# Seven block products in place of eight in part of a down projection (float32 trunk kernel, one Trainium2 core)

## The chip, the core and the metric

One NeuronCore of a Trainium2 chip runs the whole program. The metric is the device time of one execution in microseconds (us); for the kernel before it is the median of three timed executions. Beside these stands one profiled execution, with a trace of every engine.

## The reference

Two residual layers over a sequence of 256 tokens of width 2048, all in float32. Each layer has three kinds of attention heads and then a gated MLP with a causal convolution. The change lies in the MLP's last product:

```python
def _conv_gated_mlp(h, w_up, conv_w, conv_b, w_down):
    u = jnp.einsum('bsd,df->bsf', h, w_up)
    u = lax.conv_general_dilated(u, ...) + conv_b
    a, g = jnp.split(u, 2, axis=-1)
    return jnp.einsum('bsf,fd->bsd', jax.nn.silu(g) * a, w_down)
...
        x = x + jnp.einsum('bsm,md->bsd', mix, w_o[l])
        h = _rmsnorm(x, ffn_norm[l])
        x = x + _conv_gated_mlp(h, ffn_w_up[l], ffn_conv_w[l], ffn_conv_b[l], ffn_w_down[l])
    return _rmsnorm(x, final_norm)
```

D_FF is 5632, so `w_down` is 5632 x 2048 in each of the two layers.

## The kernel before, in words

**Weights as a stream.** The host packs all weights into blocks of 128x128 in the order of their use. SyncE's queue brings them in chunks of 16 blocks (1 MB, tile `raw`, three buffers, `load`, L109). Each half of a chunk (128x1024, called a sub-chunk here) is split for TensorE by `convert` (L128): ScalarE casts it to `hi` (L140), VectorE subtracts, `lo = raw - hi` (L141, called the residue here). `hi` and `lo` have five buffers each, so a sub-chunk can be cast when TensorE has finished with the one five places earlier. `weights` (L146) asks for the next sub-chunks as TensorE moves on.

**Products.** A float32 product is three TensorE matmuls: high by high, high by low, low by high. In the up projection `mm_t` (L183) takes the weights as the stationary operand, 16 matmuls with 512 columns and 16 with 256 for one output tile. In the down projection `mm_v` (L237, matmuls L249, L250, L251) takes the activations (128x128) as the stationary operand and 512 columns of weights as the moving one.

**The MLP's order.** The 5632 inner columns are done in two halves of 22 tiles. For each tile `mm_t` runs twice, VectorE adds the two parts (L261), GpSimd multiplies by the norm (L824), ScalarE and VectorE do the convolution (L827 to L829), and `to_hl` (L509) splits the result into high and low. Then `residual` (L456) does the half's down projection: for each of four column slices of 512, `mm_v` runs over the 22 tiles and both token halves into two PSUM banks, 528 matmuls in all, and VectorE adds each bank to the residual stream `xr` (L461, tiles x_77 and x_78 for the token halves).

**What follows a down projection.** After a layer's first half comes the up projection of the second half, which doesn't read the new `xr`. After the second half of layer 0 comes layer 1's norm: `RowNorm.add` (L421) squares the new rows on ScalarE, and `RowNorm.turn` (L425) transposes a column slice of `xr` on TensorE, scales it on ScalarE (L435) and takes its residue on VectorE (L436). The turns of three slices stand inside the last `residual`, that of the fourth inside layer 1's first product `mm_t2` (L220, L579). After the second half of layer 1 come the final norm and the output: GpSimd has multiplied three of the four slices by the gain (L853) as they became ready, and `put` (L859) scales eight tiles and sends them out.

**What sets the order.** The program is written in one order and a scheduler places every instruction on its engine's queue; `tc.high_priority(offset=AHEAD)` lets a piece be placed earlier. Each engine then works through its own queue in that order, and a waiting instruction holds all behind it. PSUM has eight banks: tag `mm` 3, `s` 2, `pt` 1, `pv` 1, `misc` 1. The four tags beside `mm` belong to attention and the norms, and the down projection before uses `mm` alone.

## Time and profile before

| what | value |
|---|---|
| median of 3 runs | 2251.39 us (2250.98 to 2251.55) |
| the profiled execution | 2251.53 us; its span 2249.8 us, the rest lies around it |
| TensorE busy | 2236.4 us, 99% of the span, granted clock 0.999 |
| VectorE (DVE) busy | 1487.6 us, 66% |
| ScalarE (ACT) busy | 1204.2 us, 54% |
| GpSimd (POOL) busy | 404.7 us, 18% |
| DMA | 183 GB/s read over the span |

In the profile PE is TensorE's matmuls, PEld its weight loads, DVE, ACT, POOL and SP the other engines; L141 is a line of the kernel. A matmul's shown duration includes its way through the array, so matmuls overlap in the list; how many fit into a time is read from the distance of their starts. A timeline row gives start, duration, engine, line, operation, and in brackets the idle time of the engine before it with what ended it. A row with "x2" is two instructions merged.

### The profile page before, as it was taken

Reading aid. Unit: us, or ns where it says so; the run is one execution under the profiler, and the core shown is the slowest. Engines: PE = TensorE matmul, PEld = TensorE weight load, DVE = VectorE, ACT = ScalarE, POOL = GpSimd, SP = SyncE. Lnnn points to the kernel's source line nnn. Section 1 sums busy time; section 2 is a strip of 40 time slices with the busy share of each in tenths; the row PEclk is TensorE's granted clock in tenths of the full one; section 3 lists DMA queues with packets and bytes.
Section 4 is the critical chain, followed back from the end, with each engine's and each line's share of the span. In section 5 each row is a group of like instructions: output and inputs, shape, how many; then the busy total and the mean of one; then the engine's idle time right before and its main releaser. Section 6 shows DMA issues by size and latency. Waiting matters only on the chain.

```text
span 2249.8 us, 31033 instructions
## 1 busy us (share of the span) xinstructions
PE 2236.4 (99%) x12083; PEld 1929.6 (86%) x12083; DVE 1487.6 (66%) x2317; ACT 1204.2 (54%) x1867; POOL 404.7 (18%) x395
## 2 busy tenths in 40 slices
PE   9999999999999999999999999999999999999998
PEld 8888978888888888888888889788888888888886
DVE  8767766677764577775574787566666546777653
ACT  7455645555543455554454565455555435555543
POOL 4600000222210022210050110003333101222210
PEclk9999999999999999999999999999999999999999
DMA  8544445455555555555555444355555555555653
GB/s 314 200 160 159 156 141 181 162 194 194 187 206 189 186 189 187 190 202 188 187 182 193 150 167 159 131 185 178 186 185 185 207 200 187 188 187 187 208 201 114
DMA packets 60915, 413.59 MB, mean 184 GB/s; under 512 B 6880, under 2 KB 7008, under 8 KB 11744
## 3 DMA queue, kind: packets, MB, share of 16 engines
q1 hardware_dynamic: 60048, 410.54, 51.6%
q8 instruction: 95, 1.56, 0.3%
q10 hardware_dynamic: 720, 1.07, 0.1%
q14 instruction: 52, 0.43, 0.1%
HBM read 409.49 MB, written 2.10 MB: 183 GB/s over the span
## 4 chain that ended last, share of the span: by engine, by line
PE 98%; ACT 1%; DVE 0%; DMA 0%; issue 0%; DVEq 0%; SPq 0%; ACTq 0%
PE mm L195 37%; PE mm L200 19%; PE mm L249 12%; PE mm L250 12%; PE mm L251 12%; PE s L473 2%; PE mm L234 1%; PE mm L766 1%; PE mm L767 1%; PE mm L768 1%; PE pv L505 1%; PE mm L232 1%; PE s L432 0%; PE misc L376 0%; PE pv L506 0%; ACT hi L140 0%
## 5 line engine op out<-in xcount | busy, mean ns | idle before, releaser
L141 DVE TENSOR_TENSOR lo<-raw,hi 128x1024 fp32r<-128x1024 f32 (+1 forms) x776 | 974.9, 1264 | 499.4 <-ACT hi L140 461.0
L140 ACT CAST hi<-raw 128x1024 fp32r<-128x1024 f32 (+1 forms) x776 | 800.5, 1039 | 475.7 <-PE mm L251 367.1
L195 PE MATMUL mm<-h,hi 128*128 128x512 f32 x3584 | 863.8, 392 | 0.0
L195 PEld LDWEIGHTS mm<-h,hi 128*128 128x128 f32 x3584 | 664.7, 188 | 135.6 <-ACT tmp L259 1.3
L200 PEld LDWEIGHTS mm<-h,lo 128*128 128x128 f32 x3584 | 460.6, 190 | 13.6
L200 PE MATMUL mm<-h,lo 128*128 128x256 f32 x3584 | 465.4, 283 | 0.0
L249 PE MATMUL mm<-hi,slot 128*128 128x512 f32 x992 | 387.7, 391 | 0.0
L251 PE MATMUL mm<-hi,slot 128*128 128x512 f32 x992 | 384.8, 388 | 0.0
L250 PE MATMUL mm<-lo,slot 128*128 128x512 f32 x992 | 384.7, 388 | 0.0
L824 POOL TENSOR_TENSOR tmp<-tmp,rstd 128x256 f32<-128x256 f32 x176 | 193.4, 1099 | 1037.7 <-DVE tmp L261 727.7
L827 ACT ACTIVATE tmp<-tmp,par 128x256 f32<-128x256 f32 x176 | 106.0, 602 | 312.1 <-POOL tmp L824 312.1
L249 PEld LDWEIGHTS mm<-hi,slot 128*128 128x128 f32 x992 | 186.3, 188 | 41.5 <-issue 4.0
L251 PEld LDWEIGHTS mm<-hi,slot 128*128 128x128 f32 x992 | 186.2, 188 | 38.2
L250 PEld LDWEIGHTS mm<-lo,slot 128*128 128x128 f32 x992 | 186.3, 188 | 36.8
L828 DVE SCALAR_TENSOR_TENSOR tmp<-tmp,par,tmp 128x255 f32<-128x255 f32 x176 | 84.5, 480 | 150.7 <-ACT tmp L827 150.7
L259 ACT COPY tmp<-mm 128x256 f32<-128x256 f32 (+1 forms) x233 | 85.9, 369 | 62.1 <-PE mm L195 34.1
L832 POOL TENSOR_TENSOR tmp<-tmp,tmp 128x256 f32<-128x256 f32 x88 | 75.6, 859 | 211.6 <-ACT tmp L831 209.3
L261 DVE TENSOR_TENSOR tmp<-mm,tmp 128x256 f32<-128x256 f32 (+1 forms) x233 | 97.4, 418 | 5.5 <-ACT tmp L259 5.3
L829 DVE SCALAR_TENSOR_TENSOR tmp<-tmp,par,tmp 128x254 f32<-128x254 f32 x176 | 85.0, 483 | 6.2
L831 ACT ACTIVATE tmp<-tmp 128x256 f32<-128x256 f32 x88 | 36.8, 418 | 61.8 <-DVE tmp L829 61.7
L249 PE MATMUL mm<-hi,h 128*128 128x512 f32 (+1 forms) x192 | 68.3, 356 | 0.0
L251 PE MATMUL mm<-hi,h 128*128 128x512 f32 (+1 forms) x192 | 67.9, 354 | 0.0
(193 smaller groups left out, 1470.9 us busy)
## 6 DMA issues: line engine op xcount, KB each, us to landing
raw<-in_w SPq DMA_DIRECT2D x381, 1024.0 KB, 4.8
raw<-in_w SPq DMA_DIRECT2D x14, 256.0 KB, 5.3
slot<-in_x SPq DMA_DIRECT2D x8, 256.0 KB, 5.2
x<-in_xn SPq DMA_DIRECT2D x2, 1024.0 KB, 10.7
slot<-in_fin SPq DMA_DIRECT2D x4, 256.0 KB, 6.2
out<-x SPq DMA_DIRECT2D x4, 256.0 KB, 3.9
out<-x ACTq DMA_DIRECT2D x4, 256.0 KB, 4.0
par<-in_par SPq DMA_DIRECT2D x1, 325.0 KB, 7.6
```

Of the source, the lines that this page charges most:

```text
L140: nc.scalar.copy(hi[:, a], src[:, a])
L141: nc.vector.tensor_tensor(lo[:, a], src[:, a], f(hi[:, a]), ALU.subtract)
L195: nc.tensor.matmul(ps, ws[i][0], moving[i], start=(i == 0), stop=bool(flip and i == k - 1))
L200: nc.tensor.matmul(ps[:, :T], ws[i][1], moving[i][:, :T], start=False, stop=(not flip and i == k - 1))
L249: nc.tensor.matmul(ps[t][:, :n], s_hi, hi, start=(i == 0), stop=False)
L250: nc.tensor.matmul(ps[t][:, :n], s_hi, lo, start=False, stop=False)
L251: nc.tensor.matmul(ps[t][:, :n], s_lo, hi, start=False, stop=(i == k - 1))
L259: nc.scalar.copy(t[:rows], ps[:rows, T : 2 * T])
L261: nc.vector.tensor_tensor(u[:rows], ps[:rows, :T], t[:rows], ALU.add)
L824: nc.gpsimd.tensor_tensor(uu, u, rstd, ALU.mult)
L827: nc.scalar.activation(y, uu, AF.Identity, scale=q_[:, w + 2 : w + 3], bias=q_[:, w + 3 : w + 4])
L829: nc.vector.scalar_tensor_tensor(y[:, 2:], uu[:, : T - 2], q_[:, w : w + 1], y[:, 2:], ALU.mult, ALU.add)
```

## The change

In each half of the down projection the loop is turned around. Instead of four column slices of 512 there are two groups of 1024 columns, and in a group eleven pairs of inner tiles follow each other. A pair is a 2x2 block product: two tiles of activations, each with two token halves, by two rows and two column slices of weights (one chunk). For seven pairs it is done in eight block products, as before. For pairs 3, 6, 8 and 10 it is done in seven, by Strassen's identity: four sums of weight blocks, four differences of activation blocks, seven products, each into a bank of its own, and a final recombination in each group. A product is three matmuls, as before.

- `prepare` (VectorE): one 128x1024 and two 128x512 additions per seven-product chunk make the weight sums `t13` and `t24` (tag `sum`, two buffers). `convert` now also splits sums: a seven-product chunk has four sub-chunks (128x1024, 128x512, 128x1024, 128x1024) instead of two.
- `seven_forms`: four GpSimd subtractions of 128x128 per such pair in the up projection, and four casts and four residues instead of two.
- `down` replaces `residual` for the MLP. It uses all eight PSUM banks: products "d" and 2 in `s`, 3 in `pt`, 4 in `pv`, 1, 5 and 7 in `mm`, 6 in `misc`. At the end of each group: one ScalarE copy of bank 1 into a tile u, eight VectorE additions that read one bank each, and four GpSimd additions of u and v to `xr`.
- Layer 1's first product now starts with the turns of slices 0 and 1, and has those of 2 and 3 inside. For the final norm, GpSimd multiplies slices 0 and 1 by the gain, VectorE does 2 and 3 in `put`.
- `tmp` has 14 buffers instead of 15; the final gain lies in the `h` buffers.

```diff
+PAIRS = HALF // 2
+SEVEN = (3, 6, 8, 10)
...
+        if at in sevens:
+            bounds += [(c, 0, 4, 8), (c, 0, 12, 4), (c, 1, 0, 8), (c, 2, 0, 8)]
+        else:
+            bounds += [(c, 0, i, min(SUB, n - i)) for i in range(0, n, SUB)]
...
+    def prepare(s):
+        if s >= len(bounds) or chunks[bounds[s][0]][0] not in sevens or bounds[s][0] in sums:
+            return
...
+        nc.vector.tensor_tensor(
+            t13.rearrange(g, q=2), r[:, 1024:2048].rearrange(g, q=2),
+            r[:, 0:512].rearrange(g, q=1).to_broadcast([P, 2, 512]), ALU.add,
+        )
+        nc.vector.tensor_tensor(t24[:, :512], t13[:, :512], r[:, 1536:2048], ALU.add)
+        nc.vector.tensor_tensor(t24[:, 512:], t24[:, :512], r[:, 512:1024], ALU.add)
...
+    def step(s):
+        convert(s)
+        convert(s + 1)
+        with tc.high_priority(offset=AHEAD):
+            convert(s + 2)
+            load(bounds[s][0] + 1)
+            load(bounds[s][0] + 2)
+            prepare(s + 3)
+            prepare(s + 4)
+        return subs[s]
...
+    def down(acts, norm=None, after=None):
+        for g in range(2):
...
+            tags = {"d": ("s", 2), 2: ("s", 2), 3: ("pt", 1), 4: ("pv", 1), 1: ("mm", 3), 5: ("mm", 3), 7: ("mm", 3), 6: ("misc", 1)}
...
+                nc.tensor.matmul(banks[m], xh, hi, start=fresh, stop=False)
+                nc.tensor.matmul(banks[m], xh, lo, start=False, stop=False)
+                nc.tensor.matmul(banks[m], xl, hi, start=False, stop=last)
...
+                if p in SEVEN:
+                    last = p == SEVEN[-1]
+                    step(s)
+                    prod(2, part(a[0], 1), quad(s, 0), last)
+                    prod(1, part(a[0], 0), quad(s, 1), last)
+                    step(s + 1)
+                    prod(3, part(a[2], 1), quad(s + 1, 0), last)
+                    step(s + 2)
+                    prod(5, part(a[1], 0), quad(s + 2, 0), last)
+                    prod(7, part(a[2], 0), quad(s + 2, 1), last)
+                    step(s + 3)
+                    prod(6, part(a[1], 1), quad(s + 3, 0), last)
+                    prod(4, part(a[3], 0), quad(s + 3, 1), last)
+                else:
...
+            with tc.high_priority(offset=AHEAD):
+                add(xr[1][:, c2], xr[1][:, c2], banks["d"], ALU.add)
+                u = slot()
+                nc.scalar.copy(u, banks[1])
+                add(xr[0][:, c1], xr[0][:, c1], banks[2], ALU.add)
+                add(xr[0][:, c2], xr[0][:, c2], banks[3], ALU.add)
+                nc.gpsimd.tensor_tensor(xr[0][:, c1], xr[0][:, c1], u, ALU.add)
+                v = slot()
+                add(v, banks[6], u, ALU.add)
+                add(u, banks[5], v, ALU.subtract)
+                add(v, banks[7], v, ALU.add)
+                nc.gpsimd.tensor_tensor(xr[0][:, c2], xr[0][:, c2], u, ALU.add)
+                add(u, banks[5], v, ALU.subtract)
+                nc.gpsimd.tensor_tensor(xr[1][:, c1], xr[1][:, c1], v, ALU.add)
+                add(xr[1][:, c1], xr[1][:, c1], banks[4], ALU.add)
+                nc.gpsimd.tensor_tensor(xr[1][:, c2], xr[1][:, c2], u, ALU.add)
...
+    def seven_forms(both):
...
+        sub = nc.gpsimd.tensor_tensor
+        sub(s1, x21, x22, ALU.subtract)
+        sub(s3, x11, x21, ALU.subtract)
+        sub(s2, s1, x11, ALU.subtract)
+        sub(s4, x12, s2, ALU.add)
...
-            first = mm_t2(hx, {4: lambda: norm.turn(3), KT // 2: norm.cols})
+            norm.turn(0)
+            norm.turn(1)
+            first = mm_t2(hx, {3: lambda: norm.turn(2), 6: lambda: norm.turn(3), KT // 2: norm.cols})
...
-                residual(acts, 0, norm.turn)
+                down(acts, norm)
...
-        if j == 3:
-            nc.vector.scalar_tensor_tensor(x, x, c, gf[3], ALU.mult, ALU.mult)
-        elif t == 0:
-            nc.vector.tensor_scalar(x, x, c, None, ALU.mult)
+        if j >= 2:
+            nc.vector.scalar_tensor_tensor(x, x, c, gf[j], ALU.mult, ALU.mult)
```

**How the instructions stand.** First VectorE's queue in the first down projection. Before, where a column slice ends, the two additions of L461 stand between residues (names: `x_77`, `x_78` the residual stream, `mm` the banks, `lo` a residue):

```order
L141 TENSOR_TENSOR lo_6602<-raw_6567,hi_6601 128x1024
L461 TENSOR_TENSOR x_77<-x_77,mm_6391 128x512
L461 TENSOR_TENSOR x_78<-x_78,mm_6392 128x512
L141 TENSOR_TENSOR lo_6620<-raw_6567,hi_6619 128x1024
L141 TENSOR_TENSOR lo_6636<-raw_6605,hi_6635 128x1024
```

After, the same queue where the first group ends (L182 is the residue, L569 to L578 the recombination, L141 and L145 are `prepare`; `slot_6862` is u, `slot_6867` is v; `raw_6792`, `raw_6826` and `raw_6880` are the next group's first three chunks):

```order
L182 TENSOR_TENSOR lo_6852<-raw_6792,hi_6851 128x1024
L182 TENSOR_TENSOR lo_6877<-raw_6826,hi_6876 128x1024
L569 TENSOR_TENSOR x_77<-x_77,pt_6452 128x512
L572 TENSOR_TENSOR slot_6867<-misc_6586,slot_6862 128x512
L182 TENSOR_TENSOR lo_6897<-raw_6826,hi_6896 128x1024
L573 TENSOR_TENSOR slot_6862<-mm_6574,slot_6867 128x512
L182 TENSOR_TENSOR lo_6915<-raw_6880,hi_6914 128x1024
L574 TENSOR_TENSOR slot_6867<-mm_6578,slot_6867 128x512
L141 TENSOR_TENSOR sum_6920<-raw_6918 128x1024
L576 TENSOR_TENSOR slot_6862<-mm_6574,slot_6867 128x512
L578 TENSOR_TENSOR x_78<-x_78,pv_6470 128x512
```

Residues and a weight sum of the next group now stand between the additions that free the banks, and the one that frees `pv` comes last. GpSimd's four additions have a queue of their own, where nothing else stands at that time.

Second, TensorE's queue where layer 0 passes into layer 1. Before (`h_9597` and `h_9598` are norm outputs made during the down projection):

```order
L251 MATMUL mm_10237<-hi_10392,slot_9594 128x512
L231 MATMUL mm_10448<-h_9597,hi_10408 128x512
L232 MATMUL mm_10448<-h_9597,lo_10409 128x256
L231 MATMUL mm_10449<-h_9597,hi_10408 128x512
L232 MATMUL mm_10449<-h_9597,lo_10409 128x256
L232 MATMUL mm_10448<-h_9598,lo_10409 128x256
```

After, with equal rows shown once (L526 is the group's last product, L479 a transpose of a turn, L278 to L281 are `mm_t2`, L242 is `mm_t`; `h_9803` is the first norm output):

```order
L526 MATMUL pv_10296<-hi_10660,slot_9800 128x512
L479 MATMUL s_10710<-cs,x_77 128x128
L479 MATMUL s_10710<-cs,x_78 128x128
L479 MATMUL s_10719<-cs,x_77 128x128
L479 MATMUL s_10719<-cs,x_78 128x128
L278 MATMUL mm_10746<-h_9803,hi_10667 128x512
L279 MATMUL mm_10746<-h_9803,lo_10668 128x256
L278 MATMUL mm_10747<-h_9803,hi_10667 128x512
L279 MATMUL mm_10747<-h_9803,lo_10668 128x256
L279 MATMUL mm_10746<-h_9804,lo_10668 128x256
```

The transposes that lay inside the down projection now stand between it and the first matmul that reads a norm output, and the later turns stand between the k steps of that product.

Third, VectorE's queue at the end of the program. Before:

```order
L141 TENSOR_TENSOR lo_20524<-raw_20477,hi_20523 128x1024
L461 TENSOR_TENSOR x_77<-x_77,mm_20384 128x512
L461 TENSOR_TENSOR x_78<-x_78,mm_20385 128x512
L441 TENSOR_REDUCE rcol_20569<-sums_19793 128x2
L443 RECIPROCAL rcol_20569<-rcol_20569 128x2
L865 TENSOR_SCALAR x_77<-x_77,rcol_20569 128x512 x3
```

After (L488 and L490 are the norm, as L441 and L443 before):

```order
L182 TENSOR_TENSOR lo_21158<-sum_21095,hi_21157 128x1024
L568 TENSOR_TENSOR x_77<-x_77,s_20790 128x512
L569 TENSOR_TENSOR x_77<-x_77,pt_20779 128x512
L572 TENSOR_TENSOR slot_21182<-misc_20913,slot_21177 128x512
L573 TENSOR_TENSOR slot_21177<-mm_20901,slot_21182 128x512
L574 TENSOR_TENSOR slot_21182<-mm_20905,slot_21182 128x512
L576 TENSOR_TENSOR slot_21177<-mm_20901,slot_21182 128x512
L578 TENSOR_TENSOR x_78<-x_78,pv_20797 128x512
L488 TENSOR_REDUCE rcol_21199<-sums_20315 128x2
L490 RECIPROCAL rcol_21199<-rcol_21199 128x2
L1019 SCALAR_TENSOR_TENSOR x_77<-x_77,rcol_21199,gf_20309 128x512
```

Two additions before the norm have become a chain of seven, with four GpSimd additions beside it.

More of the change, by code (lines that the diff above doesn't have):

```diff
@@ L64, in chunk_list, with seven_starts @@
     return out
+def seven_starts():
+    per = KT * 39 + 84 + 16 * KT + 3 * FT * KT
+    out = set()
+    for l in range(DEPTH):
+        for half in range(2):
+            at = l * per + KT * 39 + 84 + 16 * KT + half * 3 * HALF * KT + 2 * HALF * KT
+            out |= {at + (g * PAIRS + p) * CH for g in range(2) for p in SEVEN}
+    return out
 @with_exitstack
@@ L87, in tmp @@
     def tmp():
-        return work.tile([P, T], F32, tag="tmp", name=nm("tmp"), bufs=15)
+        return work.tile([P, T], F32, tag="tmp", name=nm("tmp"), bufs=14)
     def small(n):
@@ L105 @@
     raws, subs = {}, {}
-    bounds = [(c, i, min(SUB, n - i)) for c, (at, n) in enumerate(chunks) for i in range(0, n, SUB)]
-    sub_of = {chunks[c][0] + o + i: (s, i) for s, (c, o, n) in enumerate(bounds) for i in range(n)}
+    sevens = seven_starts()
+    bounds = []
+    for c, (at, n) in enumerate(chunks):
+        if at in sevens:
+            bounds += [(c, 0, 4, 8), (c, 0, 12, 4), (c, 1, 0, 8), (c, 2, 0, 8)]
+        else:
+            bounds += [(c, 0, i, min(SUB, n - i)) for i in range(0, n, SUB)]
+    sub_of, sub_at = {}, {}
+    for s, (c, form, o, n) in enumerate(bounds):
+        sub_at.setdefault(chunks[c][0], s)
+        if chunks[c][0] not in sevens:
+            sub_of.update({chunks[c][0] + o + i: (s, i) for i in range(n)})
+    sums = {}
+    def prepare(s):
+        if s >= len(bounds) or chunks[bounds[s][0]][0] not in sevens or bounds[s][0] in sums:
+            return
+        c = bounds[s][0]
+        load(c)
+        r = raws[c]
+        t13 = wpool.tile([P, 1024], F32, tag="sum", name=nm("sum"), bufs=2)
+        t24 = wpool.tile([P, 1024], F32, tag="sum", name=nm("sum"), bufs=2)
+        g = "p (q n) -> p q n"
+        nc.vector.tensor_tensor(
[4 more added lines that the diff above has]
+        nc.vector.tensor_tensor(t24[:, 512:], t24[:, :512], r[:, 512:1024], ALU.add)
+        sums[c] = (t13, t24)
     def load(c):
@@ L130, in convert @@
             return
-        c, o, n = bounds[s]
+        c, form, o, n = bounds[s]
         load(c)
+        prepare(s)
         o = o * P
-        src = raws[c][:, o : o + n * P]
+        src = (sums[c][form - 1] if form else raws[c])[:, o : o + n * P]
         hi = wpool.tile([P, SUB * P], F32R, tag="hi", name=nm("hi"), bufs=5)
@@ L148, in weights @@
         if o == 0:
-            convert(s)
-            convert(s + 1)
-            with tc.high_priority(offset=AHEAD):
-                convert(s + 2)
-                load(bounds[s][0] + 1)
-                load(bounds[s][0] + 2)
+            step(s)
         o *= P
@@ L265 @@
     cs = const.tile([P, C_W], F32, tag="cs", name="cs")
-    pint = work.tile([P, T], I32, tag="tmp", name="pint", bufs=15)
+    pint = work.tile([P, T], I32, tag="tmp", name="pint", bufs=14)
     xr = [big.tile([P, D], F32, tag=f"x{t}", name=f"x{t}") for t in range(2)]
@@ L831 @@
                 nc.scalar.activation(ys[1], ys[1], AF.Silu)
-                nc.gpsimd.tensor_tensor(ys[0], ys[0], ys[1], ALU.mult)
-                a = slot(F32R)
-                to_hl(a, ys[0])
-                acts.append(a)
+                if i // 2 in SEVEN:
+                    if i % 2 == 0:
+                        both = slot()
+                    nc.gpsimd.tensor_tensor(both[:, i % 2 * T : (i % 2 + 1) * T], ys[0], ys[1], ALU.mult)
+                    if i % 2:
+                        acts.append(seven_forms(both))
+                else:
+                    nc.gpsimd.tensor_tensor(ys[0], ys[0], ys[1], ALU.mult)
+                    a = slot(F32R)
+                    to_hl(a, ys[0])
+                    if i % 2 == 0:
+                        acts.append([])
+                    acts[-1].append(a)
             if half == 0:
-                residual(acts, 0)
+                down(acts)
             elif l < DEPTH - 1:
@@ L840 @@
                 norm = RowNorm(pr[l + 1][:, Q_AN : Q_AN + KT], hx)
-                residual(acts, 0, norm.turn)
+                down(acts, norm)
             else:
-                gf = [slot() for _ in range(4)]
+                gf = [big.tile([P, 2 * T], F32, tag=f"h{k}", name=nm("gf")) for k in range(4)]
                 for j in range(4):
```

69 lines of the change are left out of this document (64 added, 5 removed).

## The prediction

> **What bounds the kernel now.** I read the page's chain of waits first, then the start and end of one down projection in TensorE's timeline.
>
> ```profile
> span 2249.8 us, 31033 instructions
> PE 98%; ACT 1%; DVE 0%; DMA 0%; issue 0%; DVEq 0%; SPq 0%; ACTq 0%
> 637.52 0.40 PE L249 MATMUL mm<-hi,slot 128*128 128x512 f32 x1
> 757.23 0.39 PE L195 MATMUL mm<-h,hi 128*128 128x512 f32 x1
> 757.46 2.08 PE L200 MATMUL mm<-h,lo 128*128 128x256 f32 x16
> 759.37 3.82 PE L195 MATMUL mm<-h,hi 128*128 128x512 f32 x16
> 637.50:757.20 119.70, 119.70 (x530) 99.13 (x529) 61.80 (x59) 48.80 (x50) 1.84 (x2) 1.00 0.57 201
> ```
>
> 98% of the chain is TensorE. The first half's 528 matmuls lie between 637.52 and 757.23: 119.71 us, 0.2267 us each, without a gap, and the up projection follows at once. In that stretch (last row: PE, PEld, DVE, ACT, POOL busy) VectorE works 61.8 and ScalarE 48.8 of 119.7 us. So a matmul less is 0.2267 us less, if nothing then makes TensorE wait. 16 matmuls of 256 columns take 759.37 - 757.46 = 1.91 us, so one `mm_t` takes 16 x 0.2267 + 1.91 = 5.54 us.
>
> **What is removed.** Eight groups with four seven-product chunks each save one product of three matmuls per chunk: 96 x 0.2267 = **21.8 us**. The queue of the change confirms the count: 2016 matmuls in `down` for 2112.
>
> **What VectorE gets.** The next rows are VectorE's and ScalarE's.
>
> ```profile
> 666.04 1.23 DVE L141 TENSOR_TENSOR lo<-raw,hi 128x1024 fp32r<-128x1024 f32 x1 [1.50 <-ACT hi L140]
> 667.18 1.28 DVE L461 TENSOR_TENSOR x<-x,mm 128x512 f32<-128x512 f32 x2
> L461 DVE TENSOR_TENSOR x<-x,mm x64: 679/680/689, 305.0 to 2239.0; 128x512 f32<-128x512 f32 x64
> 1125.14 1.05 ACT L140 CAST hi<-raw 128x1024 fp32r<-128x1024 f32 x1 [1.67 <-PE mm L251]
> 1126.10 0.63 ACT L423 ACTIVATE slot<-x 128x512 f32<-128x512 f32 x1
> raw<-in_w SPq DMA_DIRECT2D x381, 1024.0 KB, 4.8
> ```
>
> A residue takes 667.18 - 666.04 = 1.14 us of its queue, a 512-wide operation 1.28 - 0.68 = 0.60, a cast 0.96. An ordinary chunk then costs VectorE 2 x 1.14 = 2.3 us against 24 x 0.2267 = 5.4 on TensorE. A seven-product chunk costs 3 x 1.14 + 0.60 for residues and, taking the weight sums at the price of a subtraction of the same shape, 1.14 + 2 x 0.60: 6.4 us against 21 x 0.2267 = 4.8. A group: 4 x 6.4 + 7 x 2.3 + 8 x 0.60 = 46 us against 252 x 0.2267 = 57.1. Inside a group this is covered: five buffers let VectorE run ahead, and from pair 6 to pair 10 (three of the dear chunks, two ordinary ones) it needs 23.8 us while TensorE works 25.2. The sums need a landed chunk; the 4.8 us of a load fit in as well, since a `raw` buffer is freed about one chunk before TensorE reaches it. ScalarE's 3.5 casts (3.4 us) are hidden under 4.8. I take **0** inside a group. The new operations of `seven_forms` lie in the up projection under 11.1 us of matmuls per tile: 0.
>
> **GpSimd holds VectorE.** The ends of groups need the price of GpSimd's additions.
>
> ```profile
> 2210.88 2.97 POOL L853 TENSOR_TENSOR x<-x,slot 128x512 f32<-128x512 f32 x2 [26.96 <-ACT slot L423]
> 2212.98 1.95 DVE L141 TENSOR_TENSOR lo<-raw,hi 128x1024 fp32r<-128x1024 f32 x1 [1.54 <-ACT hi L140]
> 2215.71 1.23 DVE L141 TENSOR_TENSOR lo<-raw,hi 128x1024 fp32r<-128x1024 f32 x1 [0.78 <-ACT hi L140]
> L853 POOL TENSOR_TENSOR x<-x,slot x6: 1289/1502/1714, 2151.0 to 2212.6; 128x512 f32<-128x512 f32 x6
> L261 DVE TENSOR_TENSOR tmp<-mm,tmp x233: 405/418/426, 30.5 to 2119.8; 128x256 f32<-128x256 f32 x115, 70x256 f32<-70x256 f32 x2
> ```
>
> A GpSimd addition of 128x512 takes 1.29 us alone (the smallest of L853; 1.25 between starts is my estimate). A residue that starts while it runs takes 1.95 instead of 1.23 us: it ends at 2214.93, 1.08 after GpSimd's end at 2213.85, so it was held until about then. VectorE's additions from a PSUM bank show no such stretch (none of L261's 233 is over 0.426), so I let them run beside GpSimd.
>
> The Trainium skill says this in "SBUF — State Buffer", "Who interferes with whom": a VectorE instruction with two SBUF inputs and a GpSimd one that reads SBUF block each other, whichever issues second, and one with at most one SBUF input doesn't contend. The stretched residue agrees; that the bank additions go free no row here proves, and if they were held too, about 1.5 us would come on top at each of seven group ends.
>
> **Between the two groups of a half (four times).** Let 0 be the time when the last product is issued. The first sub-chunk of pair 10 is free 15 matmuls earlier (-3.4, plus 0.2 until the last has run through). Casts follow at 0.96, so residue `lo_6852` ends at -0.95 and `lo_6877` at 0.2. Then, by the queue shown above: bank 3 to 0.8, v to 1.4. GpSimd's first addition, held by the residue, runs 0.2 to 1.45. `lo_6897` waits for it: 1.45 to 2.6; u to 3.2; `lo_6915` to 4.35; v to 4.95. GpSimd's second runs 4.35 to 5.6, the weight sum is held and runs to 6.75, GpSimd's third 6.75 to 8.0, u to 7.35; the last addition must follow GpSimd's third on the same tile: 8.65. TensorE's queue asks for bank `pv` after 34 matmuls, at 7.7. Wait: 1.0 us. The same tally gives 1.6 for the second such place (there the copy of bank 1 stands ahead of a cast, so that GpSimd starts at -0.95 and holds the next residue), 1.0 for the third and, with 29 matmuls of cover and no weight sum ahead, 1.0 for the fourth: **4.6 us** (0 if GpSimd's holding costs half, 10 if each bank is 1.4 later).
>
> **Down to up (twice).** Here the second `mm_t` needs the bank of product 5, at 5.54. Its second reader is behind two residues and GpSimd's second addition: u first at 4.95, v 5.55, a residue held until 6.35 and run to 7.5, u again 8.1. Wait 2.6, twice: **5.3 us** (2.6 to 7.6).
>
> **Layer 0 to 1 (once).**
>
> ```profile
> 1124.94 0.39 PE L231 MATMUL mm<-h,hi 128*128 128x512 f32 x1
> 1127.93 1.04 PE L432 MATMUL s<-cs,x 128*128 128x128 f32 x8
> 1137.29 0.61 PE L376 MATMUL misc<-tmp,cs 128*128 128x128 f32 x4
> 1127.45 1.28 ACT L442 ACT_TABLE_LOAD   x1
> 1129.88 0.83 ACT L435 ACTIVATE h<-s,par 128x256 fp32r<-128x256 f32 x2
> ```
>
> Before, 1137.29 - 1124.94 = 12.35 us without a gap, with one turn (8 transposes, 0.11 us each) inside. After, all four turns lie here: 12.35 + 24 x 0.11 = 15.0 us of work, and three were in the down projection before, so work is unchanged. But TensorE, after 8 transposes (0.9 us), waits for the first norm output. ScalarE makes it after a cast and a squaring, VectorE's part comes behind v at 4.2, and the second output bank is product 5's, free at 5.1. From there ScalarE sets the pace: 16 scalings x 0.4, 4 squarings x 0.63, 4 casts x 0.96, the 1.28 table load, about 14 us in all, and 4 us of waiting for GpSimd's last additions in front of the squarings. Following both queues I come to 22.3 us, of which 2.1 is work done early for the next product: 20.2 - 15.0 = **5.2 us** (3 to 8).
>
> The Trainium skill's "TensorE: Matmul & The Clock Gate", "Part 1: The HAM clock gate", speaks against this place: an idle window of about 3.4 us halves TensorE's clock until a busy one has passed. By it the 4.3 us without matmuls would cost up to 1.7 us more; no such gap lies before the program's end here. ScalarE would hide part of it, and I leave it to the range.
>
> **The end (once).**
>
> ```profile
> 2238.62 0.39 PE L251 MATMUL mm<-hi,slot 128*128 128x512 f32 x1
> 2239.09 0.63 ACT L423 ACTIVATE slot<-x 128x512 f32<-128x512 f32 x1 [12.59 <-DVE x L461]
> 2240.53 0.16 DVE L441 TENSOR_REDUCE rcol<-sums 128x2 f32<-128x8 f32 x1 [0.79 <-ACT slot L423]
> 2241.31 1.33 ACT L867 ACTIVATE x<-x,rcol 128x512 f32<-128x512 f32 x2 [0.29 <-DVE rcol L443]
> ```
>
> With 0 at 2238.85, the reduction stands at 1.7 and the first output scaling at 2.5. After: v from bank 6 at 0.15, u 0.75, v 1.35, GpSimd's second 0.85 to 2.1, u 2.75, GpSimd's third to 3.35, bank 4 at 4.0, GpSimd's fourth to 4.6; three squarings (0.63) from 4.1 end at 6.1, so the reduction is at 6.2 and the outputs begin at 7.0. Eight scalings then take as long as before on two engines. **4.7 us** (4 to 6).
>
> **Sum.** -21.8 + 4.6 + 5.3 + 5.2 + 4.7 = -2.0 us on 2251.53: **2249.5 us**. The profiled execution lies 0.14 above the median, so I leave it there. With all low ends (0 + 2.6 + 3 + 4 = 9.6) it is 2239; with all high ends (10 + 7.6 + 8 + 6 = 31.6) 2261. Within 0.2%, about 4.5 us, a measurement of this kernel can't tell a change from none, so this forecast is "the same".
>
> **Rivals.**
> - *The matmuls come back nearly whole.* If VectorE stands earlier than I have it at the group ends, only the low ends are paid: 2239. For it: the waits are short against 7.7 us of cover in TensorE's queue, and half a microsecond decides each. Against: the end and the layer change can't be covered, nothing else is left to do there. 30%.
> - *VectorE becomes the bound.* Rows with GpSimd busy show dear residues (1.95). At 1.35 a residue or sum and 0.68 a short operation a group costs 4 x 7.5 + 7 x 2.7 + 8 x 0.68 = 54 and with 5 us of GpSimd's additions 59 against 57.1. From a residue price of 1.3 on it decides: 8 x 2.2 = 17.6 of waits inside groups, on top of 5.3, 5.2 and 4.7: 2251.5 - 21.8 + 32.8 = 2262.5. For it: 46 of 57 leaves little in a queue that must wait for casts, loads and GpSimd. Against: the down projection's own residues take 1.23, and GpSimd stands still inside a group. 28%.
> - *It does not save the matmuls:* excluded by the count.
>
> The forecast has 42%. The range takes in both rivals' figures, 2239 to 2263; the likeliest case alone reaches from 2246 to 2256. Faster 0.30, same 0.42, slower 0.28.
>
> **What would show it.** Right: in the changed profile 12 matmuls fewer per group with 0.2267 between starts, TensorE idle 1 to 2 us before the first `pv` product of each second group, about 2.6 before the second `mm_t` after a half, some 4 behind the transposes at the layer change, and 15.6 us from the last matmul to the span's end instead of 10.9. Wrong: TensorE waiting for residues or sums inside a group, a weight sum far from 1.14 us, no wait for a bank at all, or longer up projections.

## The result, and the profile after

| what | before | after |
|---|---|---|
| median | 2251.2 us (4 executions) | 2292.5 us (3) |
| profiled execution; its span | 2251.53; 2249.8 us | 2292.54; 2290.8 us |
| TensorE's granted clock | 0.999 | 0.992 |

The ratio of the two times is 1.0184, 95% interval 1.0170 to 1.0197: slower by 41.3 us. The forecast of 2249.5 and its range (2239 to 2263) are both missed. Of the kernel after's four timed executions three lie between 2291.7 and 2293.7 us; the fourth took 7850.4 us for a reason that stays open and is left out here, while the expectations below reckon with 2293.1, the median of all four.

First the page of the kernel after: its chain, then five groups of the list of waits (engine, tile and line that waited, releaser: us in total, times, longest).

```profile
span 2290.8 us, 31330 instructions
PE 49%; DVE 8%; POOL 6%; ACT 4%; issue 3%; DMA 1%; DVEq 0%; ACTq 0%; POOLq 0%
```

```profile
DVE sum L141 <- DMA raw<-in_w: 25.2, 12, 3.5
ACT slot L653 <- POOL slot L643: 17.3, 16, 1.5
PE misc L525 <- DVE lo L182: 16.4, 4, 4.2
DVE slot L654 <- ACT slot L653: 13.9, 14, 1.1
PE mm L247 <- DVE lo L182: 9.8, 10, 1.7
```

TensorE was 98% of the chain and is 49% now. It waits for residues in two places that I had priced at nothing: four times over 4 us inside a group (`misc` is the bank of product 6), and ten times in the up projection (L247). VectorE itself waits for landed chunks with weight sums, and for ScalarE's copies in `seven_forms`, which wait for GpSimd.

A stage here runs from the start of a down projection's first matmul to that of its last; the kernel before is in brackets. The first half's down projection begins at 644.22 (637.52), the four take 122.7, 124.1, 121.8 and 124.2 us (119.5, 122.2, 119.5, 119.5), and from the last matmul to the span's end it is 16.0 (11.1). 24 matmuls fewer per half should have made 114.0 of 119.5.

The 41.0 us between the spans add up so: -21.8 for the matmuls; waits of TensorE over 0.4 us, read from the distance of its starts: 17.1 in pair 3 of the four first groups, 3.6 just ahead of these, 11.5 in the up projections, 3.6 between groups, 4.7 at the layer change, 2.4 in the last group; 4.9 at the end. That makes 26.0. What is left, 15, must be slower matmuls and waits under 0.4 us. The next rows show what slower matmuls are: two windows of the kernel after (us, busy of PE, PEld, DVE, ACT, POOL, then the granted clock), one up to the end of the first long wait and one behind it.

```profile
640.00:670.50 30.50, 25.52 (x116) 20.27 (x116) 19.07 (x26) 16.47 (x24) 7.90 (x9) 1.00 0.48 170
670.50:673.90 3.40, 3.40 (x9) 2.63 (x8) 3.40 (x5) 1.04 (x1) 0.00 (x0) 0.50 0.00 0
```

And the timeline there, VectorE and TensorE:

```profile
662.07 0.69 DVE L182 TENSOR_TENSOR lo<-raw,hi 128x512 fp32r<-128x512 f32 x1
663.02 1.23 DVE L182 TENSOR_TENSOR lo<-sum,hi 128x1024 fp32r<-128x1024 f32 x1 [0.26 <-ACT hi L181]
665.57 0.40 PE L524 MATMUL misc<-hi,slot 128*128 128x512 f32 x1
667.78 1.22 DVE L141 TENSOR_TENSOR sum<-raw 128x1024 f32<-128x1024 f32 x1 [3.53 <-DMA raw<-in_w]
668.92 1.22 DVE L182 TENSOR_TENSOR lo<-sum,hi 128x1024 fp32r<-128x1024 f32 x1
670.19 0.55 PE L525 MATMUL misc<-lo,slot 128*128 128x512 f32 x1 [4.23 <-DVE lo L182]
670.54 0.63 PE L526 MATMUL misc<-hi,slot 128*128 128x512 f32 x1
670.96 0.63 PE L524 MATMUL pv<-hi,slot 128*128 128x512 f32 x1
671.39 0.63 PE L525 MATMUL pv<-lo,slot 128*128 128x512 f32 x1
```

TensorE's product 6 of pair 3 needs the residue of 668.92. That residue stands on VectorE's queue behind the weight sum of pair 6 (L141), and the sum waits 3.53 us for a load. The load took the `raw` buffer that the residue of 662.07 was the last to read. After the wait matmuls start 0.43 us apart (670.96, 671.39) instead of 0.2267, for one window of 3.4 us at half clock.

The up projection's waits start like this (timeline behind tile 7, the second of pair 3):

```profile
561.13 1.47 DVE L182 TENSOR_TENSOR lo<-raw,hi 128x1024 fp32r<-128x1024 f32 x1 [1.49 <-ACT hi L181]
561.59 1.31 POOL L643 TENSOR_TENSOR slot<-slot,slot 128x128 f32<-128x128 f32 x1
562.94 0.41 ACT L653 CAST slot<-slot 128x256 fp32r<-128x256 f32 x1 [1.53 <-POOL slot L643]
563.25 0.36 ACT L306 COPY tmp<-mm 128x256 f32<-128x256 f32 x1
563.65 0.42 DVE L308 TENSOR_TENSOR tmp<-mm,tmp 128x256 f32<-128x256 f32 x1 [1.05 <-ACT tmp L306]
575.73 1.22 PE L247 MATMUL mm<-h,lo 128*128 128x256 f32 x8 [1.70 <-DVE lo L182]
```

GpSimd's subtraction takes 1.31 us while a residue runs on VectorE. ScalarE's copy of a combination waits for it, and the copy of the next tile's accumulator (L306) stands behind that. So the next tile's whole chain (accumulator, norm on GpSimd, convolution, then the next cast and residue) is late, and one tile later TensorE waits.

### The profile page after: what moved, and what is told of

It is laid out like the page before. It is cut to its first block, busy times and chain, and to the rows that moved or that the text cites. A ratio compares the mean times of both kernels' runs of the same rounds, so it can differ in the third digit from the quotient of the medians.

```text
span 2290.8 us, 31330 instructions
## 1 busy us (share of the span) xinstructions
PE 2234.0 (98%) x11987; PEld 1918.3 (84%) x11987; DVE 1645.6 (72%) x2540; ACT 1256.0 (55%) x1972; POOL 529.4 (23%) x489
## 4 chain that ended last, share of the span: by engine, by line
PE 49%; DVE 8%; POOL 6%; ACT 4%; issue 3%; DMA 1%; DVEq 0%; ACTq 0%; POOLq 0%
PE mm L242 15%; PE mm L247 8%; DVE lo L182 3%; POOL tmp L971 3%; PE mm L296 2%; PE mm L298 2%; PE mm L297 2%; PE s L525 2%; PE s L526 2%; PE s L524 2%; PE pv L524 1%; ACT hi L181 1%; PE pv L526 1%; PE pv L525 1%; ACT tmp L974 1%
## 5 line engine op out<-in xcount | busy, mean ns | idle before, releaser
L182 DVE TENSOR_TENSOR lo<-raw,hi 128x1024 fp32r<-128x1024 f32 (+1 forms) x776 | 942.3, 1229 | 242.4 <-ACT hi L181 225.4
L181 ACT CAST hi<-raw 128x1024 fp32r<-128x1024 f32 (+1 forms) x776 | 782.0, 1020 | 333.5 <-PE mm L298 122.2
L242 PE MATMUL mm<-h,hi 128*128 128x512 f32 x3584 | 864.6, 393 | 0.0
L242 PEld LDWEIGHTS mm<-h,hi 128*128 128x128 f32 x3584 | 665.9, 188 | 135.4 <-ACT tmp L306 1.7
L247 PEld LDWEIGHTS mm<-h,lo 128*128 128x128 f32 x3584 | 461.9, 190 | 27.0 <-DVE lo L182 12.4
L247 PE MATMUL mm<-h,lo 128*128 128x256 f32 x3584 | 470.9, 283 | 9.9 <-DVE lo L182 9.8
L971 POOL TENSOR_TENSOR tmp<-tmp,rstd 128x256 f32<-128x256 f32 x176 | 210.0, 1193 | 774.1 <-DVE tmp L308 463.4
L296 PE MATMUL mm<-hi,slot 128*128 128x512 f32 (+1 forms) x288 | 113.6, 394 | 0.0
L298 PE MATMUL mm<-hi,slot 128*128 128x512 f32 (+1 forms) x288 | 111.0, 385 | 0.0
L297 PE MATMUL mm<-lo,slot 128*128 128x512 f32 (+1 forms) x288 | 110.8, 385 | 0.0
L181 ACT CAST hi<-sum 128x1024 fp32r<-128x1024 f32 x64 | 67.0, 1053 | 78.1 <-PE pt L526 46.2
L182 DVE TENSOR_TENSOR lo<-sum,hi 128x1024 fp32r<-128x1024 f32 x64 | 78.2, 1223 | 40.4 <-ACT hi L181 40.3
L306 ACT COPY tmp<-mm 128x256 f32<-128x256 f32 (+1 forms) x233 | 84.9, 364 | 36.9 <-PE mm L242 17.1
L525 PE MATMUL s<-lo,slot 128*128 128x512 f32 x256 | 101.3, 396 | 2.2 <-DVE lo L182 2.2
L524 PE MATMUL s<-hi,slot 128*128 128x512 f32 x256 | 101.4, 396 | 0.0
L526 PE MATMUL s<-hi,slot 128*128 128x512 f32 x256 | 101.0, 395 | 0.0
L986 POOL TENSOR_TENSOR tmp<-tmp,tmp 128x256 f32<-128x256 f32 x56 | 52.9, 945 | 129.6 <-ACT tmp L978 129.6
```

The lines of the kernel that those rows point to most:

```text
L181: nc.scalar.copy(hi[:, a], src[:, a])
L182: nc.vector.tensor_tensor(lo[:, a], src[:, a], f(hi[:, a]), ALU.subtract)
L242: nc.tensor.matmul(ps, ws[i][0], moving[i], start=(i == 0), stop=bool(flip and i == k - 1))
L247: nc.tensor.matmul(ps[:, :T], ws[i][1], moving[i][:, :T], start=False, stop=(not flip and i == k - 1))
L296: nc.tensor.matmul(ps[t][:, :n], s_hi, hi, start=(i == 0), stop=False)
L297: nc.tensor.matmul(ps[t][:, :n], s_hi, lo, start=False, stop=False)
```

## The experiments

**Sums issued late** (e1). `step` no longer issues sums; `convert` does, for summed sub-chunks only.

```diff
-        prepare(s)
+        if form:
+            prepare(s)
...
-            prepare(s + 3)
-            prepare(s + 4)
```

> The weight sums are no longer issued three and four sub-chunks ahead; each chunk's sums are issued when its first summed sub-chunk is converted (two sub-chunks ahead). Nothing else is changed. Theory A (the sum of pair 6 stands on VectorE's queue ahead of the residue for product 6 of pair 3 and waits there for a load; each such stall also halves TensorE's clock for 3.4 us): the four waits of 4.40, 4.27, 4.19 and 4.23 us go (17.1 us), and with each some 1.6 us of lost clock (3.41 us at half speed), together 6 to 8 us; the waits in the up projections stay. 2268 to 2271 us, ratio to the kernel before 1.007 to 1.009. Theory B (VectorE or ScalarE has too much work inside a group, wherever it is queued): the same work still has to be done, the waits move to another product and the time stays at 2287 to 2295, ratio 1.016 to 1.020.

2296.1 us, 1.0197 [1.0181, 1.0212]: nothing gained. But the edit missed its aim. Issuing the sum later in the program didn't move it on the queue: the sum of pair 6 still stood one row ahead of that residue (rows 848 and 849 of VectorE's queue) and waited 3.33 us. The theory wasn't tested.

**No `seven_forms`** (e2), and **both edits** (e3). These two, and e5, e6 and e8 below, leave out sums or combinations that the identity needs: they show times, and their products are of other numbers.

```diff
-                    if i % 2:
-                        acts.append(seven_forms(both))
...
+                if i // 2 in SEVEN and i % 2:
+                    acts[-1] += acts[-1][::-1]
```

> seven_forms is left out: the sevens' activations go through the ordinary copy and residue of the kernel before, and the seven products use those two activations again in place of the combinations (so these products are of other numbers). Weight sums, loop order, banks and recombination stay as in the changed kernel. Theory A (the chain GpSimd, ScalarE, VectorE in seven_forms holds VectorE up during the up projection, and leaves it late by 6 us where the down projection begins, which is what makes pair 6's load late): the up projections go back to about 245.6 us each (6 to 7, 5.5, about 3 and 2.1 us, some 17 us together), and the four stalls in pair 3 shrink to under 1.5 us each, with the clock kept: 2252 to 2262, ratio 1.000 to 1.005. Theory A2 (the stall comes from the early sums alone, whatever VectorE did before): only the 17 us of the up projections go, the four stalls stay: 2274 to 2278, ratio 1.010 to 1.012. Theory B (VectorE's amount of work): under 5 us gained.

> Both edits: sums issued late, and the ordinary copies and residues in place of seven_forms (products of other numbers). What is left of the change is 96 matmuls fewer, the sums themselves, the new loop order, the transposes that were moved, and the recombination. Theory A: no stall inside a group, up projections as before, so only the ends are paid: 2251.2 - 21.8 + 4.9 (end) + 4.7 to 6.4 (layer change with its clock) + 3.6 (between the groups) + 2.4 (GpSimd in the last half) = 2245 to 2250, ratio 0.997 to 0.9995. Theory B (VectorE's work inside a group): TensorE waits for residues somewhere in every group, 2260 or more, ratio over 1.004.

2259.3 us, 1.0031 [1.0020, 1.0042], and 2258.9, 1.0030 [1.0019, 1.0042]. In e2 the first down projection begins at 637.06, no up projection has a wait over 0.4 us, and pair 3 waits like this (TensorE, timeline of e2):

```profile
656.81 0.39 PE L524 MATMUL misc<-hi,slot 128*128 128x512 f32 x1
658.82 0.49 PE L525 MATMUL misc<-lo,slot 128*128 128x512 f32 x1 [1.62 <-DVE lo L182]
```

The sum still waits 3.46 us for its load there, but VectorE is earlier against TensorE, and 1.6 us of it show. So `seven_forms` costs 33 us: the waits in the up projections, and stalls in pair 3 of 4.2 to 4.4 us instead of 0.5 to 2.9 in the four first groups. The 2245 to 2250 for e3 were missed: waits of 0.8 to 2.8 us are left in the groups.

**Eight products in the new order** (e4), with four additions per group.

```diff
-SEVEN = (3, 6, 8, 10)
+SEVEN = ()
...
```

> No pair takes seven products (SEVEN is empty): eight products everywhere, no weight sums, no combinations, and four additions per group in place of the thirteen steps of recombination. The new loop order (two groups of 1024 columns, four banks), the banks and the moved transposes and norm steps stay. The rival theory C (it is the new order that costs): it shows here without the seven products: 2251.2 + 4 to 5 (end) + 5 to 6.5 (layer change) + 0 to 2 (between groups) = 2260 to 2265, ratio 1.004 to 1.006. If the order costs only what the recombination makes it cost, 2251 to 2256, ratio 1.000 to 1.002.

2259.9 us, 1.0036 [1.0022, 1.0049]. Every down projection takes 119.5 us; from the last matmul of layer 0 to the first down matmul of layer 1 it is 639.0 us, 629.4 before and 2.7 for the moved transposes: 6.9 lost. The end takes 12.9 us, 1.7 more than before. The new order alone costs 8.4 us.

**No sums** (e5): `convert` takes every residue from `raw`. **Neither sums nor forms** (e8): this edit and that of e2.

```diff
-        prepare(s)
-        o = o * P
-        src = (sums[c][form - 1] if form else raws[c])[:, o : o + n * P]
+        o = (o, 8, 0)[form] * P
+        src = raws[c][:, o : o + n * P]
...
-            prepare(s + 3)
-            prepare(s + 4)
```

> No weight sums: the residues that stood on sums are taken from the raw weights (so products 6, 4, 5 and 7 are of other numbers); seven_forms, loop order and recombination stay. With the sums issued late, the sum of pair 6 still stood on VectorE's queue ahead of the residue for product 6 of pair 3, waiting 3.33 us for its load, so that experiment did not take away what it was to take away; here no sum is on the queue at all. Theory A (that residue is late because it stands behind the sum that waits): the four stalls of 4.2 to 4.4 us go with their clock windows, the up projections keep their waits: 2266 to 2272, ratio 1.006 to 1.009. Theory A2 (VectorE comes 6 us late into the down projection by the chain of seven_forms, and this alone makes the residue late): the stalls stay over 2 us each, 2280 to 2290, ratio 1.013 to 1.017.

> No seven_forms and no weight sums (products of other numbers): what is left of the change is the 96 matmuls fewer, the loop order and the recombination at the end of each group. Theory A: 2251.5 - 21.8 + 8.4 (the loop order, measured with eight products) + 3.1 (the end beyond that, 16.0 against 12.9) + 4.2 (waits between the groups) + 1 to 2 (gain multiplications on GpSimd) = 2246 to 2249, ratio 0.9975 to 0.999; and so the sums alone cost 10 to 13 us (2258.9 with them, no forms). Theory B (sums are free, the rest of the 20 us is the recombination): 2256 to 2260, ratio 1.002 to 1.004.

2261.6 us, 1.0045 [1.0028, 1.0062], and 2246.25, 0.9974 [0.9964, 0.9983]. Windows of the first down projection, e5 and e8:

```profile
644.33:759.27 114.94, 114.33 (x505) 94.36 (x504) 79.62 (x82) 63.37 (x72) 13.34 (x12) 1.00 0.57 201
```

```profile
637.43:752.37 114.94, 114.33 (x505) 94.35 (x504) 77.88 (x78) 62.00 (x68) 10.77 (x8) 1.00 0.57 201
```

e5 begins as late (644.33) as the changed kernel, and yet its groups run at full clock, with no wait over 0.4 us but the one for a bank between them (0.77). So being late does no harm by itself inside a group, and a sum that waits does less by itself (e2). Over e8 the forms cost 15.3 us, the sums 13.0 (e2), both 46.3: about 18 of it only because they meet.

**Copies without GpSimd's additions** (e6; the four lines that call `sub` are out, and `e = both`), and **the additions on VectorE** (e9):

```diff
-        sub = nc.gpsimd.tensor_tensor
+        sub = nc.vector.tensor_tensor
```

> seven_forms without GpSimd's four additions: its four copies and four residues are kept, and read the activations in place of the combinations (products of other numbers). Sums, order and recombination stay. It splits what seven_forms costs (2293.1 with it, 2259.3 without). Theory A (GpSimd's additions are the slow link: ScalarE's copies wait for them and VectorE's residues for the copies): most comes back, 2259 to 2268, ratio 1.003 to 1.007. Rival D (what costs is that pairs of tiles are converted together, four copies and four residues behind the second tile of a pair, so that the queues of ScalarE and VectorE are put in another order; GpSimd adds little): over 2280, ratio over 1.013.

> seven_forms issues its four 128x128 additions on VectorE in place of GpSimd; all else is the changed kernel. Theory A (the handovers GpSimd to ScalarE to VectorE are the slow link, and cost 21.5 of the 34 us: 2293.1 with them, 2271.6 with the copies and residues alone): no wait over 0.8 us in the up projections, the 4.2 to 4.4 us stalls partly kept since the sums stay: 2270 to 2280, ratio 1.008 to 1.013. Rival B (VectorE's amount of work is the bound, so 64 more small additions on it make it worse): 2293 or more, ratio 1.018 or more.

2271.6 us, 1.0089 [1.0074, 1.0104], and 2285.6, 1.0156 [1.0140, 1.0171], each above theory A's figure and under its rival's. GpSimd's four small additions cost 21 of the 33 us. On VectorE they are cheaper, but the residue of the next weights then stands behind them, and they wait for the tile's product: waits of 0.5 to 1.2 us in the up projections, 3.4 to 3.6 in pair 3.

**Forms in the down projection** (e7), two pairs ahead of their use.

```diff
+                if g == 0 and p + 2 in SEVEN:
+                    acts[p + 2] = seven_forms(acts[p + 2])
                 a = acts[p]
...
```

> All of seven_forms is issued in the first group of the down projection, two pairs ahead of the pair that uses it; the up projection issues only the product of the two halves of each tile into the pair's buffer. Same work, later place: the queues show all sixteen residues of the forms between the last tiles of the up projection and the first pairs, in place of four behind each of tiles 7, 13, 17 and 21. Theory A (the forms' chain behind tiles 7, 13 and 17 makes the 1.86 us waits in the up projections): no wait over 0.5 us in the up projections, down projections at 121 to 125 us as now: 2275 to 2283, ratio 1.010 to 1.014. Rival D (VectorE then comes still later into the down projection): stalls of 6 us and more in the first pairs, 2290 or more, ratio 1.017 or more.

2293.6 us, 1.0183 [1.0168, 1.0198]. Up projections as before (the first down projection begins at 638.63), but 128.2 us for it. The loss moved, as rival D said, though not into stalls of 6 us: this half has four of 1.4 to 2.4 us.

**One buffer for both sums** (e12).

```diff
-        t13 = wpool.tile([P, 1024], F32, tag="sum", name=nm("sum"), bufs=2)
-        t24 = wpool.tile([P, 1024], F32, tag="sum", name=nm("sum"), bufs=2)
+        both = wpool.tile([P, 2048], F32, tag="sum", name=nm("sum"), bufs=1)
+        t13, t24 = both[:, :1024], both[:, 1024:]
```

> The two sums of a chunk share one buffer of 2048 columns, and there is one such buffer in place of two of 1024: the sum of pair 6 can then not be queued ahead of the residue that reads the sum of pair 3, so it stands one place later on VectorE's queue, behind that residue and ahead of the residues of pair 4. Nothing else moves there. Theory A (the residue is late because it stands behind a sum that waits for its load): product 6 of pair 3 no longer waits over 1 us, and the wait turns up with pair 4's first products, 2.5 to 4 us, since the sum still waits for the same load: 2282 to 2294, ratio 1.013 to 1.019. Theory A2 (VectorE is late by its own work): product 6 waits as before.

2291.8 us, 1.0182 [1.0167, 1.0197]. TensorE's timeline of e12 at the same place:

```profile
665.74 0.39 PE L525 MATMUL misc<-lo,slot 128*128 128x512 f32 x1
665.96 0.39 PE L526 MATMUL misc<-hi,slot 128*128 128x512 f32 x1
...
666.87 0.39 PE L524 MATMUL s<-hi,slot 128*128 128x512 f32 x1
670.63 0.79 PE L525 MATMUL s<-lo,slot 128*128 128x512 f32 x1 [3.37 <-DVE lo L182]
```

One place on VectorE's queue, and the wait moved by just the products that lie between: product 6 goes through, pair 4's first product waits. This shows the stall to be the sum's place on an in-order queue.

**The sevens moved** (e10), **also with the additions on VectorE** (e11, with e9's edit).

```diff
-SEVEN = (3, 6, 8, 10)
+SEVEN = (3, 5, 7, 9)
...
```

> The sevens are pairs 3, 5, 7 and 9 in place of 3, 6, 8 and 10 (and the end flag of each bank goes to its last product): the same number of products, sums and combinations. The last pair is then an ordinary one, so the last tile of the up projection has the ordinary copy and residue, products 1, 5, 6 and 7 are complete one pair before the group's end, and the chunk whose sum stood waiting is two chunks ahead of the residue it stands before, not three. Theory A (order in the queues): no stall over 1.5 us in pair 3, no wait between groups, end at 12.9 to 14 us, up projections as now: 2256 to 2266, ratio 1.002 to 1.0065. Rival B (amount of work): stalls somewhere else in the group, 2280 or more, ratio over 1.012.

> Both: the sevens at pairs 3, 5, 7 and 9 and the four additions of seven_forms on VectorE. Theory A: the gains add, less what the two have in common: 2247 to 2257, ratio 0.998 to 1.0025. Rival B: 2275 or more, ratio over 1.010.

2277.7 us, 1.0121 [1.0105, 1.0138], and 2277.7, 1.0118 [1.0103, 1.0133]. The long stall is gone (under 1.3 us in pair 3), which gives 15 us. The rest was missed: the order in which I add the banks was left alone, so the wait between groups grew to 1.9 us and the end to 16.6; and the up projections' waits are still there. e11 lies at rival B's figure: with the sevens moved, the additions on VectorE gain nothing, against 7 us in e9.

**Forms two tiles later** (e13; e10's sevens, the forms behind the next pair's second tile), **and the additions on VectorE** (e17).

```diff
+                if i % 2 and i // 2 - 1 in SEVEN:
+                    acts[i // 2 - 1] = seven_forms(acts[i // 2 - 1])
                 nc.scalar.activation(ys[1], ys[1], AF.Silu)
...
```

> The kernel with the sevens at pairs 3, 5, 7 and 9, and each pair's seven_forms issued two tiles later (behind the second tile of the next pair) instead of at once. The queues then show ScalarE's copy of the next tile's accumulator ahead of the forms' copies that wait for GpSimd, and VectorE's residues of the forms behind the next tile's convolution. Same work. Theory A (order: the next tile's work stands behind a copy that waits for GpSimd): no wait over 0.8 us in the up projections, which go back to about 246 us each; 2277.7 less 15 to 19 = 2259 to 2263, ratio 1.003 to 1.005. Rival B (amount of work on VectorE and ScalarE): the waits stay, over 2272, ratio over 1.009.

> Sevens at pairs 3, 5, 7 and 9, seven_forms two tiles later, as the kernel at 2287.5, but its four additions on VectorE. In that kernel GpSimd's additions stood ahead of the next tile's multiplication on GpSimd's own queue (busy from 549.92 to 555.25, the multiplication ready at 552.5 and begun at 554.51). Theory A (GpSimd's additions are in the loop of the next tile, wherever they are placed on its queue): the waits of 1.9 to 2.4 us in the up projections fall under 1.2 us, 2268 to 2277, ratio 1.008 to 1.011. Rival B (VectorE's amount of work in the up projections): they stay or grow, 2287 or more, ratio over 1.0155.

e13 was a miss, and slower than e10: 2287.5 us, 1.0159 [1.0142, 1.0176]. GpSimd's timeline of e13:

```profile
549.92 0.74 POOL L988 TENSOR_TENSOR tmp<-tmp,tmp 128x256 f32<-128x256 f32 x1 [2.54 <-ACT tmp L980]
550.61 0.47 POOL L641 TENSOR_TENSOR slot<-slot 128x128 f32<-128x128 f32 x1
551.03 1.45 POOL L642 TENSOR_TENSOR slot<-slot 128x128 f32<-128x128 f32 x1
552.45 0.69 POOL L643 TENSOR_TENSOR slot<-slot,slot 128x128 f32<-128x128 f32 x1
553.22 1.32 POOL L644 TENSOR_TENSOR slot<-slot,slot 128x128 f32<-128x128 f32 x1
554.51 0.74 POOL L971 TENSOR_TENSOR tmp<-tmp,rstd 128x256 f32<-128x256 f32 x1
```

The additions now hold the next tile's multiplication (L971), whose input was ready at about 552.5. With them on VectorE (e17): 2270.4 us, 1.0084 [1.0069, 1.0099], as forecast; the waits of 1.9 to 2.4 us are 0.7 to 1.3. So in both places that were tried, GpSimd's additions hold up a tile's own chain: in the kernel after through ScalarE's copies, in e13 on GpSimd's queue.

**Sums on GpSimd** with sevens at 4, 6, 8, 9 (e14), **three sevens** at 4, 6, 8 (e15), **sums on VectorE** (e16, sevens as e14): all with e13's edit and with the complete products added first. **e18** is e15 with e9's edit.

```diff
-        nc.vector.tensor_tensor(
+        nc.gpsimd.tensor_tensor(
             t13.rearrange(g, q=2), r[:, 1024:2048].rearrange(g, q=2),
...
```

> Sevens at pairs 4, 6, 8 and 9, seven_forms two tiles later, the weight sums on GpSimd (first one behind the last tile's chain), and the recombination ordered so that products 1, 5, 6 and 7, complete before the last pair, are added first and the four banks last. Theory A: nothing is left but the matmuls saved (21.8), the loop order (8.4, measured with eight products) and remains of 1 to 4 us per half: 2240 to 2250, ratio 0.995 to 0.9995. Rival E (GpSimd is too slow for the sums: 4 us and more for each chunk's 2048 columns, and VectorE slows it): TensorE waits for residues of sums inside the groups, 2260 or more, ratio over 1.004.

> As the kernel with later forms and sums on GpSimd, but three sevens in place of four (pairs 4, 6 and 8): 72 matmuls fewer than before in place of 96, 16.3 us in place of 21.8. Theory A: 5.4 us slower than with four, 2246 to 2255. If GpSimd's sums are the limit (rival E), three sevens with a pair between them are faster than four: under 2258 while the four give over 2260.

> As the kernel with later forms and sums on GpSimd, but the sums stay on VectorE. It tells what the sums cost there once nothing else is late. Theory A (order): 2 to 8 us over the one with sums on GpSimd, 2245 to 2256. Rival B (VectorE's amount of work inside a group, 6.9 us a seven against TensorE's 4.8): 10 us and more over it, waits of 1 us and more in several pairs of each group, 2257 or more.

> The kernel with three sevens, forms two tiles later and sums on GpSimd (2265.4), with the four additions of seven_forms on VectorE: the version that the runs so far point to. Theory A: the down projections stay at 116 to 117 us and the up projections lose half of their 15 us: 2254 to 2261, ratio 1.001 to 1.0045. Rival B: 2265 or more, ratio over 1.006. That it beats the kernel before (under 2247) would need up projections as before and a shorter change of layer, and is not expected.

2307.9 us, 1.0251 [1.0236, 1.0266]; 2265.4, 1.0063 [1.0048, 1.0078]; 2271.75, 1.0091 [1.0076, 1.0106]; e18 2254.6, 1.0014 [1.0004, 1.0024]. GpSimd's groups in e14:

```profile
L141 POOL TENSOR_TENSOR sum<-raw 128x1024 f32<-128x1024 f32 x32 | 88.8, 2776 | 115.8 <-DMA raw<-in_w 78.5 <-DVE lo L182 37.3
L146 POOL TENSOR_TENSOR sum<-sum,raw 128x512 f32<-128x512 f32 x32 | 64.6, 2020 | 2.5
L145 POOL TENSOR_TENSOR sum<-sum,raw 128x512 f32<-128x512 f32 x32 | 63.8, 1995 | 7.1 <-DVE lo L182 4.9
```

A chunk's sums take GpSimd 2.78 + 2.02 + 2.00 = 6.8 us, and two sevens in a row (pairs 8 and 9) leave it 4.8: rival E. So e14 is slower than e16, and the comparison that was to size the sums on VectorE failed. e16 has waits of 0.7 to 1.3 us for residues and casts in its groups, as its rival B (VectorE's amount of work) said; no run tells there between that and the order on the queue. e15 missed its figures as well. With GpSimd doing the sums and a pair between the sevens the down projections are nearly free of waits (first and last one of e18, windows):

```profile
642.75:759.07 116.32, 116.02 (x512) 95.41 (x510) 101.26 (x79) 60.50 (x67) 58.87 (x29) 1.00 0.58 207
2124.28:2239.81 115.53, 115.53 (x510) 95.49 (x509) 94.88 (x75) 59.12 (x71) 65.88 (x33) 1.00 0.51 178
```

510 matmuls without a wait, 509 distances of 0.2267, would make 115.4. e18, as forecast, is the best version found that computes the whole product, and it is still 3 us over the kernel before: 7 us in layer 0's up projections, 7 at the layer change and 1.4 at the end outweigh the 13 net of the down projections. Only e8 is under the kernel before, and it leaves out the sums and combinations.

## Why the prediction was wrong, point by point

- *"I take 0 inside a group"* is the step that failed first. The tally of VectorE's work was nearly right: it gave 92 us for a half's two groups, and the busy time is 98.0 of 122.7, with residues and sums at 1.22 to 1.28 us in the mean. Over a half, capacity was not the bound, so the rival "VectorE becomes the bound" was not it either, though its 2262.5 was nearest. What failed is the sentence that a load fits in because a buffer is freed about one chunk before it is needed: that counted from TensorE. The buffer is freed by VectorE, whose last residue of that chunk starts 17.85 us behind the first down matmul (13.71 in e2, without the forms), and what stands behind the waiting sum on VectorE's queue is a residue that TensorE needs first. Cost: 17.1 us of waits in pair 3, 3.6 ahead of them, and the half clock behind them. e5 and e12 show it.
- *"The new operations of `seven_forms` lie in the up projection under 11.1 us of matmuls per tile: 0."* This failed too: 11.5 us of waits there, and the lateness that turns the sums into stalls. I compared an amount of work with TensorE's time, and didn't follow the chain that goes through GpSimd, ScalarE and VectorE once per tile. e2, e6, e13 and e17 show it; for the part that the copies alone cost (12 us of 33) no run separates queue order from work.
- *Down to up, 5.3 us*: wrong, no wait over 0.4 us. *Between the groups, 1.0, 1.6, 1.0, 1.0*: measured 0.77, 1.28, 0.77, 0.77. *The end, 4.7*: measured 4.9 (the steps as listed add up to 4.5). These last two were followed on the queues step by step, and the bank additions ran beside GpSimd as assumed (rows at the end). A wait of 2.4 us in the last group was not forecast.
- *Layer change, 5.2 us and "up to 1.7" for the clock*: 3.35 + 1.32 us of waits, 6.9 in all. That 5.2 and 1.7 also make 6.9 is luck: the forecast put 4 us of it down to GpSimd's last additions, and e4 loses the same 6.9 without any recombination, so it belongs to the loop order.
- *The clock.* I gave the rule of the Trainium skill's "TensorE: Matmul & The Clock Gate", "Part 1: The HAM clock gate", only the layer change, since I saw no other gap. It counts more: seven windows of 3.4 us at half clock before the end, 23.9 us in all, worth at most 12. Those behind the four long waits of 4.2 to 4.4 us agree with it. One stands behind a wait of only 1.90 us (949.48), shorter than the page's idle window; there the measurement decides.
- *The Trainium skill's "SBUF — State Buffer", "Who interferes with whom"* spoke of GpSimd's additions and VectorE's residues, and I used it for the group ends alone. In the up projection it does the same: 1.31 us for a 128x128 subtraction beside a residue, 0.46 without one (L644).

## What to carry to other kernels

Work that fits into an engine's idle share is not free: ask for each added instruction which queue it is put on, what it waits for, and who waits for what stands behind it, above all where its input is a load whose buffer the same engine frees. Two small costs of this kind (13 and 15 us alone) made 46 together, since the one used up the lead that hid part of the other. Where TensorE is the bound, a wait of some microseconds can be paid a second time in clock.

## What the runs showed of the hardware

- A TensorE wait shorter than the 3.4 us of a half-clock window can have one behind it, but not each one does: the forms in the down projection (e7) have a wait of 2.1 us with half clock behind it, the changed kernel one of 2.4 us without. No run here shows what decides. First e7, timeline and windows, then the kernel after:

```profile
649.18 0.50 PE L525 MATMUL s<-lo,slot 128*128 128x512 f32 x1 [1.97 <-DVE lo L182]
```

```profile
650.00:653.40 3.40, 3.40 (x10) 2.66 (x9) 2.14 (x4) 0.79 (x2) 1.65 (x1) 0.50 0.88 308
```

```profile
2239.01 0.50 PE L525 MATMUL s<-lo,slot 128*128 128x512 f32 x1 [2.19 <-DVE lo L182]
```

```profile
2236.00:2246.00 10.00, 7.81 (x35) 6.14 (x34) 9.04 (x10) 3.06 (x4) 0.00 (x0) 1.00 0.46 166
```

- GpSimd's sums slow VectorE: the mean residue of 128x1024 from `raw` over a whole run is 1.39 us in e14 (sums on GpSimd), 1.26 in the kernel after.
- The same 128x128 addition took 0.29 us on VectorE (e11) and between 0.45 and 1.46 on GpSimd (both in e13).
- VectorE's additions that read a bank ran beside GpSimd's without being held: in the kernel after, the 24 of L574, L576 and L578 all overlap a GpSimd addition, and none is over 0.69 us, as long as the 32 of L508 that overlap none. At the program's end:

```profile
2276.09 0.69 DVE L574 TENSOR_TENSOR slot<-mm,slot 128x512 f32<-128x512 f32 x1
2276.13 1.26 POOL L575 TENSOR_TENSOR x<-x,slot 128x512 f32<-128x512 f32 x1 [2.40 <-DVE slot L573]
```
